# Trunk step on one core: in the MLP's down product, which engine begins the stores and the held back loads, SyncE's loads in the order of the source, and the two resident weight halves in each other's place

## The chip, the cores and the metric

The kernel runs on one core of a Trainium2 chip. The metric is the time of one execution on the device in microseconds (us), lower is better; "before" is the median of three runs. A profiled execution is one further run whose trace gives the rows quoted below. TensorE (PE) does the matmuls, VectorE (DVE), ScalarE (ACT) and GpSimd (POOL) the elementwise work. SyncE (SP) computes nothing: it begins DMA transfers one after the other, and while its next transfer waits for something, every transfer written behind it waits too. GpSimd can begin transfers as well, between its own instructions.

## The reference

One inference step of a two-layer trunk over 1072 columns (16 learned meta tokens, 32 new frames of a running stream, 1024 prompt frames), width 1024, in fp32. Layer 0 mixes with sliding-window attention beside a gated linear attention, layer 1 with a forgetting attention; behind each mixer stands the same MLP. The change touches the MLP alone:

```python
def mlp(h, w_up, w_down):
    u = jax.nn.relu(h @ w_up)
    return (u * u) @ w_down
...
        xp = xp + mlp(rmsnorm(xp, norm_mlp[l]), w_up[l], w_down[l])
        xs = xs + mlp(rmsnorm(xs, norm_mlp[l]), w_up[l], w_down[l])
```

`w_up` is 1024 x 4096 and `w_down` 4096 x 1024, both fp32, and different in each layer.

## The kernel before

**Arithmetic.** Each fp32 operand is split in a rounded high part (`hi_lo`, the cast of ACT at L64) and the rest (the subtraction of DVE at L66); a product is three matmuls, high times high (L75), high times low (L76) and low times high (L77). So the first matmul of a product needs only the cast of its activations, and the second one also their rest.

**Seven products for eight.** Both MLP products are done in a form that replaces a 2 x 2 block product by seven block products of sums and differences. `up` (L930 to L1003) runs through 16 blocks of 64 of the 4096 inner columns of each half, seven products each, and stores after each block seven combinations of the squared results (B11, B21, B22, T1 to T4) from a place in the residual's tile `xT` to a tensor in DRAM, `ud`, with one DMA (L1001). The residual itself was saved to DRAM (`xsave`) before.

**The down product.** `down` (L1010) reads them back. It has seven products n = 0 to 6 (weights A11, S2, S3, A22, A12, S1, S4), and each has two column halves c = 0, 1: 14 passes (n, c), written here (0,0), (0,1), (1,0) and so on. A pass has 16 steps kb of 12 matmuls each, 192 in all. Two steps share one tile of activations u: `acts` loads it (`md_ur`, three buffers) and splits it (`md_u`, four buffers), so a pass has eight such groups, g0 to g7. `ready(at)` makes the activations of a group and of the two behind it. Where the passes with c = 0 accumulate in the PSUM tiles `mu_y` and those with c = 1 in `bank`, the tile's name in a trace tells the two apart.

**Weights.** A11 and A21 stay in SBUF: `k1` and `k2`, four tiles `md_k` of 1 MB each. The other two quarters come in single steps (`md_raw`, 256 KB, three buffers). `weights(n, kb)` combines them and splits the result into `md_w`*kb*, one buffer for each step; for product n+1 it is called in pass (n,1), behind the matmuls of the same step, since these read the buffer it writes. For S2 a step takes two DVE operations (L1032 adds the raw weights to `k2`, L1033 takes `k1` off) and the split. For S3 it takes one (L1037, `k1` less the raw A21), the split, and then ACT's copy of the raw weights to `k1` (L1049), which sets the raw buffer free.

**The start and the held back loads.** Before, `down` begins with the four loads of `k1`, then makes all 16 `md_w` of the first product, and only then the first activations; the scheduler orders this as its model of time finds best. The four loads of `k2` (1 MB each) are spread over pass (0,0), and the restores of `xT` from `xsave` stand at step 4 of each pass with n below 4. Each is held back by a copy of one element by GpSimd (`behind`, L1064), which makes the target tile depend on activations that are made later.

**What sets the order.** Each engine works off its instructions in one fixed order. The program is written in a tile language whose scheduler finds that order with a model of time; only PE follows the order of the source in the MLP (`manual_schedule` in `mlp`). So SP's loads, in the kernel before, stand in the order that the scheduler found for them, and not in that of the loops. At the end of a pass with c the outputs are added to `xT` by DVE (L1120 before, L1124 after the change).

## Time and profile before

| what | value |
|---|---|
| time before, median of 3 runs | 2859.85 us (2859.53 to 2866.35) |
| the profiled execution | 2855.66 us, of which its span 2853.9 us |
| mean granted clock of TensorE | 0.963 |
| TensorE busy | 2631.2 us, 92% of the span |
| VectorE, ScalarE, GpSimd busy | 1888.3, 1264.4, 560.7 us |
| wait of TensorE ahead of the first down product, both layers together | 26.9 us |
| moved by SP's DMA queue, by GpSimd's | 383.62 MB, 7.01 MB |

A row of the timeline gives the start in us from the beginning of the span, the busy time in us, the engine, the line, the operation, the tiles written and read, the number of alike instructions in a row (x4), and in brackets the idle time of the engine just before and what ended it. `SPq` is SP's queue of DMA issues: such a row tells when SP began the transfers, not when they landed. In the view of waits the three numbers behind a pair are the us waited in total, how often, and the longest. In the view of windows come, behind a window, its length, the busy time and number of instructions of PE, PE's weight loads, DVE, ACT and POOL, then the granted clock of TensorE as a share of full speed, the share of the DMA engines, and GB/s.

### The profile page before, as it was taken

What the parts mean: (1) busy time and instruction counts of PE and PEld (TensorE: products, weight loads), DVE (VectorE), ACT (ScalarE), POOL (GpSimd) and SP (SyncE); (2) the same over time, 40 slices, a digit from 0 to 9 for tenths busy, and PEclk for the clock granted to TensorE, in tenths of its full rate; (3) what the DMA queues carried; (4) which work ended last, traced back from release to release, by engine and by line L of the source; (5) the groups of instructions that cost most, each with busy time, mean ns of one, the idle gap of its engine ahead of it and who ended that gap; (6) DMA issues with size and microseconds to landing.
All of it is one profiled execution on the core that took longest, in us unless ns stands there. A gap on an engine that the chain in (4) does not pass through costs nothing.

```text
span 2853.9 us, 49119 instructions
## 1 busy us (share of the span) xinstructions
PE 2631.2 (92%) x18391; PEld 2440.6 (86%) x18391; DVE 1888.3 (66%) x3856; ACT 1264.4 (44%) x2820; POOL 560.7 (20%) x611
## 2 busy tenths in 40 slices
PE   5899988879999899999999978999978999899998
PEld 5788966769999799999789856778768999899998
DVE  5934376687676677578643556778888666677553
ACT  4435454243333345445333346666653333335342
POOL 3423354200000010003110244555520000010000
PEclk9999988899999899999999979999988999999999
DMA  5343241143445577544465374344332444486643
GB/s 192 100 134 104 72 140 45 30 120 101 151 129 164 202 231 218 168 134 121 123 193 168 115 176 127 89 101 102 77 91 79 144 147 144 164 274 205 200 138 105
DMA packets 371286, 393.77 MB, mean 138 GB/s; under 512 B 41503, under 2 KB 300280, under 8 KB 369000
## 3 DMA queue, kind: packets, MB, share of 16 engines
q1 hardware_dynamic: 368552, 383.62, 45.6%
q0 software_dynamic: 2496, 7.01, 0.7%
q8 instruction: 145, 2.38, 0.4%
q14 instruction: 93, 0.76, 0.1%
HBM read 263.94 MB, written 125.48 MB: 136 GB/s over the span
## 4 chain that ended last, share of the span: by engine, by line
PE 63%; issue 16%; DVE 9%; DMA 3%; ACT 2%; SPq 1%; POOL 1%; DVEq 0%; ACTq 0%; POOLq 0%
PE bank L75 11%; PE bank L76 11%; PE bank L77 11%; PE mu_y L77 5%; PE mu_y L76 5%; PE mu_y L75 5%; PE bank L1470 2%; PE bank L1480 1%; PE bank L1481 1%; PE fx_s L1452 1%; PE fx_s L1453 1%; DMA md_raw<-in_w_down 1%; PE bank L257 1%; DVE gl_Q L600 1%; PE b L701 1%
## 5 line engine op out<-in xcount | busy, mean ns | idle before, releaser
L75 PE MATMUL bank<-pj_wh,h 128*128 128x384 f32 (+3 forms) x832 | 298.0, 360 | 9.4 <-ACT pj_wh L64 7.0
L77 PE MATMUL bank<-pj_wh,h 128*128 128x384 f32 (+3 forms) x832 | 295.9, 357 | 6.0 <-DVE h L66 4.8
L76 PE MATMUL bank<-pj_wl,h 128*128 128x384 f32 (+3 forms) x832 | 297.3, 358 | 3.5 <-DVE pj_wl L66 3.5
L75 PE MATMUL mu_y<-md_u,md_w 128*128 128x268 f32 (+1 forms) x896 | 259.4, 289 | 26.9 <-ACT md_u L64 26.9
L76 PE MATMUL mu_y<-md_u,md_w 128*128 128x268 f32 (+1 forms) x896 | 257.8, 288 | 2.4 <-DVE md_u L66 2.4
L77 PE MATMUL mu_y<-md_u,md_w 128*128 128x268 f32 (+1 forms) x896 | 257.3, 287 | 0.0
L75 PE MATMUL bank<-md_u,md_w 128*128 128x268 f32 (+1 forms) x896 | 257.1, 287 | 0.0
L77 PE MATMUL bank<-md_u,md_w 128*128 128x268 f32 (+1 forms) x896 | 255.2, 285 | 0.0
L76 PE MATMUL bank<-md_u,md_w 128*128 128x268 f32 (+1 forms) x896 | 254.9, 285 | 0.0
L64 ACT CAST md_u<-md_ur 128x536 fp32r<-128x536 f32 (+1 forms) x224 | 141.1, 635 | 210.7 <-PE mu_y L77 110.7
L66 DVE TENSOR_TENSOR md_u<-md_ur,md_u 128x536 fp32r<-128x536 f32 (+1 forms) x224 | 157.9, 710 | 114.2 <-ACT md_u L64 113.8
L76 PE MATMUL mu_y<-ho_T,mu_w 128*128 128x268 f32 (+1 forms) x768 | 219.8, 286 | 0.2 <-DVE ho_T L66 0.2
L77 PE MATMUL mu_y<-ho_T,mu_w 128*128 128x268 f32 (+1 forms) x768 | 219.9, 286 | 0.0
L75 PE MATMUL mu_y<-ho_T,mu_w 128*128 128x268 f32 (+1 forms) x768 | 219.2, 285 | 0.0
L75 PEld LDWEIGHTS mu_y<-md_u,md_w 128*128 128x128 f32 x896 | 171.1, 191 | 27.4 <-ACT md_u L64 27.3
L66 DVE TENSOR_TENSOR mu_w<-mu_raw,mu_w 128x512 fp32r<-128x512 f32 x160 | 110.0, 688 | 117.0 <-ACT mu_w L64 117.0
L1283 POOL TENSOR_TENSOR fx_p<-fx_p,sm_den 128x144 f32<-128x144 f32 (+7 forms) x128 | 150.6, 1177 | 181.8 <-DVE sm_den L1282 164.7
L64 ACT CAST mu_w<-mu_raw 128x512 fp32r<-128x512 f32 x160 | 99.2, 622 | 188.6 <-PE bank L77 124.6
L75 PEld LDWEIGHTS bank<-pj_wh,h 128*128 128x128 f32 x832 | 158.8, 191 | 22.3 <-ACT pj_wh L64 7.5
L76 PEld LDWEIGHTS mu_y<-md_u,md_w 128*128 128x128 f32 x896 | 170.9, 191 | 3.5 <-DVE md_u L66 3.4
L77 PEld LDWEIGHTS bank<-pj_wh,h 128*128 128x128 f32 x832 | 158.6, 191 | 17.5 <-DVE h L66 5.1
L76 PEld LDWEIGHTS bank<-pj_wl,h 128*128 128x128 f32 x832 | 159.0, 191 | 16.3 <-DVE pj_wl L66 5.2
(538 smaller groups left out, 8096.2 us busy)
## 6 DMA issues: line engine op xcount, KB each, us to landing
md_raw<-in_w_down SPq DMA_DIRECT2D x160, 256.0 KB
mu_raw<-in_w_up SPq DMA_DIRECT2D x64, 512.0 KB
ud<-xT SPq DMA_DIRECT2D x16, 1876.0 KB
md_ur<-ud SPq DMA_DIRECT2D x112, 268.0 KB
ud<-xT SPq DMA_DIRECT2D x16, 1848.0 KB
md_ur<-ud SPq DMA_DIRECT2D x112, 264.0 KB
md_k<-in_w_down SPq DMA_DIRECT2D x16, 1024.0 KB
fh_ka<-zk SPq DMA_DIRECT2D x32, 260.0 KB
```

Of the source, the lines that this page charges most:

```text
L64: nc.scalar.copy(hi, src)
L66: nc.vector.tensor_tensor(lo, src, hi.bitcast(F32), op=ALU.subtract)
L75: mm(out, ah, bh, start=start, stop=False)
L76: mm(out, ah, bl, start=False, stop=False)
L77: mm(out, al, bh, start=False, stop=stop)
L257: nc.tensor.matmul(*args, start=k == x == 0, stop=k == KB - 1 and x == 1)
L600: eng.tensor_tensor(ov, xv[r, :, :, 1], qv[r, :, :, 1], op=ALU.mult)
L701: nc.tensor.matmul(po[:m, h % 2, h // 2], att[:, h, :m], v[:, P * h:P * h + P], start=True, stop=False)
L1283: nc.gpsimd.tensor_tensor(p[:, :n], p[:, :n], den[:, 0:1].to_broadcast([P, n]), op=ALU.mult)
L1452: nc.tensor.matmul(s[:, a:b], qa[:, qc], ka[:, t0 + a:t0 + b], start=True, stop=False)
L1453: nc.tensor.matmul(s[:, a:b], qb[:, qc], kb[:, t0 + a:t0 + b], start=False, stop=ma >= mb)
L1470: nc.tensor.transpose(pt[:m, P * j:P * j + P], pr[j][:, k0:k0 + m], self.ident)
```

## The change

Six edits, all in the MLP:

1. The 16 stores of `ud` in a layer are begun by GpSimd instead of SP.
2. So are the four held back loads of `k2`.
3. So are the restores of `xT` (16 DMAs over eight passes in a layer).
4. `down` stands under `manual_schedule` for SP and GpSimd: both now follow the order of the source in it.
5. The tiles of `k2` are allocated ahead of those of `k1`, so that each half has the other's place in SBUF, over other operands of `up` than before.
6. `down` begins with the first load of `k1`, the first three loads of activations, and the other three loads of `k1`. Ahead of pass (0,0) only six of the 16 `md_w` are made; the other ten follow within that pass, each six steps ahead of its use.

The matmuls are the same, and in the same order. The diff, without what only shifts lines:

```diff
-                nc.sync.dma_start(self.ud[b // 4][:, b % 4], place[:, b % 2, 1:8, :hw])
+                nc.gpsimd.dma_start(self.ud[b // 4][:, b % 4], place[:, b % 2, 1:8, :hw])
...
-        def load(dst, x, kb, n=1):
+        def load(dst, x, kb, n=1, queue=nc.sync):
             a, c = int(x[1]) - 1, int(x[2]) - 1
-            nc.sync.dma_start(dst, wd[:, c, kb:kb + n, 512 * a:512 * a + 512])
+            queue.dma_start(dst, wd[:, c, kb:kb + n, 512 * a:512 * a + 512])
...
-        for x in range(4):
-            load(k1[x], "A11", 4 * x, 4)
...
-        for kb in range(NP):
+        load(k1[0], "A11", 0, 4)
+        ready(0)
+        for x in range(1, 4):
+            load(k1[x], "A11", 4 * x, 4)
+        for kb in range(6):
             w[0, kb] = weights(0, kb)
...
+                if n == 0 and c == 0 and kb + 6 < NP:
+                    w[0, kb + 6] = weights(0, kb + 6)
                 if n == 0 and c == 0 and kb % 4 == 2:
                     x = k2[kb // 4]
                     behind(x[0:1, 0, 0:1], u)
-                    load(x, "A21", kb - 2, 4)
+                    load(x, "A21", kb - 2, 4, nc.gpsimd)
...
-                        nc.sync.dma_start(self.xT[:, k:k + 2, c0:c1], self.xsave[:, k:k + 2, c0:c1])
+                        nc.gpsimd.dma_start(self.xT[:, k:k + 2, c0:c1], self.xsave[:, k:k + 2, c0:c1])
...
-            k1, k2 = ([kp.tile([P, 4, 512], F32, name=f"md_k{x}{y}") for y in range(4)] for x in (1, 2))
+
+            k2, k1 = ([kp.tile([P, 4, 512], F32, name=f"md_k{x}{y}") for y in range(4)] for x in (2, 1))
...
-            self.down(k1, k2, sb, ps, mid, end)
+            with tc.manual_schedule(engines={mybir.EngineType.SP, mybir.EngineType.Pool}):
+                self.down(k1, k2, sb, ps, mid, end)
```

The order of instructions shows it at three places, all in layer 0 (layer 1 has the same places). First SP's transfers from the end of `up` to the middle of pass (0,0). Before (`md_k_10197` to `10200` is `k1`, `10201` the first tile of `k2`; `ud_6540` to `ud_6543` hold four blocks of the stored results each):

```order
L1018 DMA md_k_10197<-in_w_down 128x4x512
L1018 DMA md_k_10198<-in_w_down 128x4x512
L1018 DMA md_k_10199<-in_w_down 128x4x512
L1018 DMA md_k_10200<-in_w_down 128x4x512
L1058 DMA md_ur<-ud_6540 128x2x268 x2
L1058 DMA md_ur<-ud_6541 128x2x268
L1018 DMA md_raw<-in_w_down 128x512 x2
L1001 DMA ud_6543<-xT 128x3752
L1018 DMA md_raw<-in_w_down 128x512
L1018 DMA md_k_10201<-in_w_down 128x4x512
L1058 DMA md_ur<-ud_6541 128x2x268
```

With the change (`md_k_10201` to `10204` is now `k1`):

```order
L1018 DMA md_k_10201<-in_w_down 128x4x512
L1058 DMA md_ur<-ud_6540 128x2x268 x2
L1058 DMA md_ur<-ud_6541 128x2x268
L1018 DMA md_k_10202<-in_w_down 128x4x512
L1018 DMA md_k_10203<-in_w_down 128x4x512
L1018 DMA md_k_10204<-in_w_down 128x4x512
L1058 DMA md_ur<-ud_6541 128x2x268
L1058 DMA md_ur<-ud_6542 128x2x268 x2
L1058 DMA md_ur<-ud_6543 128x2x268 x2
L1058 DMA md_ur<-ud_6540 128x2x268 x2
L1058 DMA md_ur<-ud_6541 128x2x268
L1018 DMA md_raw<-in_w_down 128x512 x2
```

The store and the load of `k2` have left SP's queue, three activation loads have moved ahead of three quarters of `k1`, and the first raw weights of S2 have moved from behind the third activation load to behind the eleventh.

Second, VectorE at the start of the down product. Before (the `md_w` rows left out are ten further ones like those shown; the last rows belong to S2):

```order
L1000 TENSOR_TENSOR xT<-xT 128x536 x4
L66 TENSOR_TENSOR md_w_10212<-md_k_10197,md_w_10212 128x512
L66 TENSOR_TENSOR md_w_10215<-md_k_10197,md_w_10215 128x512
L66 TENSOR_TENSOR md_w_10218<-md_k_10197,md_w_10218 128x512
L66 TENSOR_TENSOR md_w_10221<-md_k_10197,md_w_10221 128x512
L66 TENSOR_TENSOR md_w_10224<-md_k_10198,md_w_10224 128x512
...
L66 TENSOR_TENSOR md_w_10257<-md_k_10200,md_w_10257 128x512
L66 TENSOR_TENSOR md_u<-md_ur,md_u 128x536 x3
L1032 TENSOR_TENSOR md_k_10201<-md_k_10201,md_raw 128x512 x3
L1033 TENSOR_TENSOR md_k_10201<-md_k_10201,md_k_10197 128x512 x2
```

With the change (again ten `md_w` rows are left out):

```order
L66 TENSOR_TENSOR md_w_10229<-md_k_10201,md_w_10229 128x512
L66 TENSOR_TENSOR md_w_10232<-md_k_10201,md_w_10232 128x512
L66 TENSOR_TENSOR md_w_10235<-md_k_10201,md_w_10235 128x512
L66 TENSOR_TENSOR md_w_10238<-md_k_10201,md_w_10238 128x512
L66 TENSOR_TENSOR md_u<-md_ur,md_u 128x536 x3
L66 TENSOR_TENSOR md_w_10241<-md_k_10202,md_w_10241 128x512
...
L66 TENSOR_TENSOR md_w_10416<-md_k_10204,md_w_10416 128x512
L66 TENSOR_TENSOR md_u<-md_ur,md_u 128x536 x7
L1124 TENSOR_TENSOR xT<-xT,mu_y 128x268 x2
L66 TENSOR_TENSOR md_u<-md_ur,md_u 128x536
L1124 TENSOR_TENSOR xT<-xT,mu_y 128x268 x2
L1032 TENSOR_TENSOR md_k_10197<-md_k_10197,md_raw 128x512 x2
```

The first three splits of activations now stand behind four `md_w` instead of 16, and the first L1032 has moved behind the additions that end pass (0,0).

Third, SP's transfers in pass (1,1), where the weights of S3 are made. Before, from the load for g7 of that pass (`ud_6543`) on; the rows behind it with `ud_6540`, `ud_6540`, `ud_6541`, `ud_6541` are g0 to g3 of pass (2,0):

```order
L1058 DMA md_ur<-ud_6543 128x2x268
L1018 DMA md_raw<-in_w_down 128x512 x2
L1058 DMA md_ur<-ud_6540 128x2x268
L1018 DMA md_raw<-in_w_down 128x512
L1058 DMA md_ur<-ud_6540 128x2x268
L1018 DMA md_raw<-in_w_down 128x512
L1058 DMA md_ur<-ud_6541 128x2x268
L1018 DMA md_raw<-in_w_down 128x512 x2
L1058 DMA md_ur<-ud_6541 128x2x268
L1018 DMA md_raw<-in_w_down 128x512 x2
```

With the change, from the same load on, with the last six of the 16 raw weights of S3:

```order
L1058 DMA md_ur<-ud_6543 128x2x268
L1018 DMA md_raw<-in_w_down 128x512 x2
L1058 DMA md_ur<-ud_6540 128x2x268
L1018 DMA md_raw<-in_w_down 128x512 x2
L1058 DMA md_ur<-ud_6540 128x2x268
L1018 DMA md_raw<-in_w_down 128x512 x2
L1058 DMA md_ur<-ud_6541 128x2x268 x2
```

Of the 16 raw loads of S3, in the first order eight stand behind the load of g2 of pass (2,0) (the first of the two `ud_6541` rows; four of the eight are in the piece shown); in the second all 16 stand ahead of it.

## The prediction

> **What bounds the kernel now.** I read the page first, then TensorE's waits, then the timelines around the largest of them.
>
> ```profile
> PE 2631.2 (92%) x18391; PEld 2440.6 (86%) x18391; DVE 1888.3 (66%) x3856; ACT 1264.4 (44%) x2820; POOL 560.7 (20%) x611
> ```
> ```profile
> PE mu_y L75 <- ACT md_u L64: 26.9, 2, 13.6
> PE mu_y L76 <- DVE md_u L66: 2.4, 4, 1.2
> ```
>
> TensorE is busy for 92% of the span, so only what it waits for can be won. The first of its waits is the one this change touches: 26.9 us in two pieces, one a layer, at the start of the down product.
>
> ```profile
> 972.67 0.29 PE L77 MATMUL bank<-ho_B,mu_w 128*128 128x268 f32 x1
> 986.29 0.59 PE L75 MATMUL mu_y<-md_u,md_w 128*128 128x268 f32 x1 [13.34 <-ACT md_u L64]
> 987.36 0.59 PE L76 MATMUL mu_y<-md_u,md_w 128*128 128x268 f32 x1 [0.47 <-DVE md_u L66]
> ...
> 2485.25 0.28 PE L77 MATMUL bank<-ho_B,mu_w 128*128 128x264 f32 x1
> ...
> 2500.16 0.59 PE L76 MATMUL mu_y<-md_u,md_w 128*128 128x264 f32 x1 [0.47 <-DVE md_u L66]
> ...
> 2512.05 0.39 PE L76 MATMUL mu_y<-md_u,md_w 128*128 128x264 f32 x1 [1.15 <-DVE md_u L66]
> ```
>
> The last matmul of `up` begins at 972.67, the second of `down` (the first that needs VectorE's part of the activations) at 987.36. VectorE, ScalarE and SP say what fills the time between:
>
> ```profile
> 974.22 2.72 DVE L1000 TENSOR_TENSOR xT<-xT 128x536 f32<-128x536 f32 x4
> 976.85 9.82 DVE L66 TENSOR_TENSOR md_w<-md_k,md_w 128x512 fp32r<-128x512 f32 x16
> 986.59 1.96 DVE L66 TENSOR_TENSOR md_u<-md_ur,md_u 128x536 fp32r<-128x536 f32 x3
> 995.10 1.90 DVE L1032 TENSOR_TENSOR md_k<-md_k,md_raw 128x512 f32<-128x512 f32 x3 [6.55 <-issue]
> ...
> 2489.38 7.38 DVE L66 TENSOR_TENSOR md_w<-md_k,md_w 128x512 fp32r<-128x512 f32 x12
> 2499.40 1.94 DVE L66 TENSOR_TENSOR md_u<-md_ur,md_u 128x528 fp32r<-128x528 f32 x3
> ```
> ```profile
> 975.36 2.18 ACT L64 CAST md_w<-md_k 128x512 fp32r<-128x512 f32 x4 [4.93 <-DMA md_k<-in_w_down]
> ```
> ```profile
> 970.03 3.88 SPq L1018 DMA_DIRECT2D md_k<-in_w_down  x4
> 973.95 3.27 SPq L1058 DMA_DIRECT2D md_ur<-ud  x3
> ```
>
> The loads of `k1` begin only at 970.03, since the tiles lie over operands that `up` still reads, so ScalarE casts its first weights at 975.36. And VectorE finishes 16 `md_w` (9.82 us) before it touches the activations.
>
> **The change part by part.**
>
> *The start (new places in SBUF, new order): a gain.* With the change the first load of `k1` and three activation loads lead SP's queue, and four `md_w` instead of 16 stand ahead of the activations on VectorE. I take the loads as landed before `up` ends, so that VectorE sets the start: it leaves L1000 at 976.85 as now, four `md_w` at 9.82/16 = 0.614 us end at 979.31, and the second matmul follows 0.77 us behind the start of the split (987.36 less 986.59), at 980.08. That is 7.28 us earlier. In layer 1: 2489.38 + 4 x 0.615 = 2491.84 for 2499.40, 7.56 us. The wait of 1.15 us at 2512.05 comes from S2's additions that stood in front of an activation; they stand later now, so it goes too. Together 7.28 + 7.56 + 1.15 = **16.0 us** less. If the loads land late, the start falls back towards that of before: the bound is no gain.
>
> Does the half clock of the restart go as well?
>
> ```profile
> 2490.00:2495.00 5.00, 0.00 (x0) 0.00 (x0) 5.00 (x10) 3.72 (x8) 0.00 (x0) 0.54 1.05 386
> 2495.00:2500.00 5.00, 0.59 (x1) 0.29 (x1) 4.78 (x8) 4.46 (x9) 0.35 (x1) 0.50 1.07 383
> 2500.00:2505.00 5.00, 4.84 (x25) 4.84 (x26) 1.34 (x3) 0.12 (x1) 1.59 (x5) 0.59 1.05 390
> ```
>
> The last matmul of `up` ends at about 2485.5 and the granted clock is near a half from 2490 on, so within about 5 us. A wait of some 7 us is left (972.96 to 980.08), so the cold start, (1 - 0.59) x 5 = 2 us in the window behind it, stays: no term.
>
> *The ten other `md_w`, now in pass (0,0).* 10 x 0.614 = 6.1 us of VectorE and as many casts move under the first pass; VectorE is idle there for 6.55 us ahead of 995.10. Hidden, at nothing; without the cover it would be 6.1 us a layer. But what used that time comes later:
>
> *S2's additions: a loss.* SP in source order brings the first raw weights of S2 behind eleven activation loads, and VectorE's order has the first L1032 behind the additions that end pass (0,0), where it began at 995.10, in the middle of the pass. From there to the split of the second activations of pass (1,0), g1, the new order has on VectorE 36 operations of weights, seven of activations and four additions to `xT`.
>
> ```profile
> 1060.24 1.55 DVE L1120 TENSOR_TENSOR xT<-xT,mu_y 128x268 f32<-128x268 f32 x4 [0.46 <-PE mu_y L77]
> ```
> ```profile
> 1037.42 0.29 PE L75 MATMUL mu_y<-md_u,md_w 128*128 128x268 f32 x1
> ...
> 1061.15 0.29 PE L75 MATMUL bank<-md_u,md_w 128*128 128x268 f32 x1
> ```
>
> A pass lasts 1061.15 - 1037.42 = 23.73 us, a group of two steps 2.97. The additions end 0.64 us (1060.24 + 1.55 - 1061.15) into the next pass. Then 36 x 0.614 + 7 x 1.96/3 + 4 x 1.55/4 = 28.2 us: g1 is split at 28.9, and TensorE wants it at 23.73 + 2.97 = 26.7. Late by 2.2; g2 stands six operations on (5 x 0.614 + 0.65 = 3.7 us, against 2.97), 0.7 more. **2.9 us** a layer, from 1 (the shorter step from one start to the next, 0.61, and less waiting) to 5 (raw loads late as well).
>
> *S3's raw weights: the larger loss.* In pass (1,1) each raw buffer is free again only when ScalarE has copied it to `k1` (L1049). Steps 0, 3, 6, 9 and 12 share one buffer:
>
> ```profile
> 1065.40 0.62 ACT L1049 COPY md_k<-md_raw 128x512 f32<-128x512 f32 x1
> ...
> 1071.73 0.62 ACT L1049 COPY md_k<-md_raw 128x512 f32<-128x512 f32 x1
> ...
> 1077.32 0.62 ACT L1049 COPY md_k<-md_raw 128x512 f32<-128x512 f32 x1 [0.22 <-DVE md_w L66]
> ...
> 1083.14 0.62 ACT L1049 COPY md_k<-md_raw 128x512 f32<-128x512 f32 x1 [0.21 <-DVE md_w L66]
> ...
> 1092.11 0.62 ACT L1049 COPY md_k<-md_raw 128x512 f32<-128x512 f32 x1 [0.86 <-DVE md_w L66]
> ```
> ```profile
> 1072.38 0.33 SPq L1018 DMA_DIRECT2D md_raw<-in_w_down  x1
> 1072.96 0.38 SPq L1058 DMA_DIRECT2D md_ur<-ud  x1
> 1074.41 0.33 SPq L1018 DMA_DIRECT2D md_raw<-in_w_down  x1
> 1074.83 0.39 SPq L1058 DMA_DIRECT2D md_ur<-ud  x1
> ...
> 1092.76 0.34 SPq L1018 DMA_DIRECT2D md_raw<-in_w_down  x1
> ```
> ```profile
> 1075.21 0.69 DVE L1037 TENSOR_TENSOR md_k<-md_k,md_raw 128x512 f32<-128x512 f32 x1 [0.45 <-DMA md_raw<-in_w_down]
> ```
> ```profile
> L64 ACT CAST md_u<-md_ur 128x536 fp32r<-128x536 f32 (+1 forms) x224 | 141.1, 635 | 210.7 <-PE mu_y L77 110.7
> ```
>
> Three steps take 5.6 to 6.3 us there (8.97 in the last link, across the end of the pass), TensorE wants three in 3 x 23.73/16 = 4.45. The chain falls behind, and raw load 15 goes out at 1092.76, behind the copy of step 12. Today that hurts nobody: g2 of pass (2,0) was loaded at 1074.83, long ahead. In source order g2 stands *behind* raw load 15, and SP waits there. By this chain: 1092.76 + 0.34, landing 2.83 later (1072.38 to 1075.21, a load of nearly that size), cast and rest 0.64 + 0.65: ready at 1097.2. TensorE wants it at 1061.15 + 23.73 + 2 x 2.97 = 1090.8. Late by 6.4 us. With all links as the first three, (1083.14 - 1065.40)/3 = 5.9, the copy of step 12 begins 3.1 us earlier: late by 3.3. I take **5.0 us** a layer, between the two; with links of the bare parts (2.83 + 0.69 + 0.62 + 0.69 + 0.62 = 5.45) it is 1.5, and 9 where they average 7.3.
>
> By the Trainium skill ("TensorE: Matmul & The Clock Gate", Part 1), TensorE falls back to half its clock after an idle window of about 3.4 us; the clock rows above agree. If S3's delay came as one wait, not over several groups as I expect, that rule would add another cold start, and the sum would be about 2 us a layer higher.
>
> *Stores, `k2` and `xT` on GpSimd.* The copies and issues that the trace has there:
>
> ```profile
> L1064 POOL COPY xT<-md_u x64: 173/174/4267, 987.4 to 2665.3; 1x1 f32<-1x1 f32 x64
> L391 POOL DMA_DIRECT2D zb<-sw_z x36 | 20.4, 566 | 55.6 <-ACT sw_z L387 35.9 <-ACT sw_es L458 12.4 <-ACT sw_z L390 7.3
> ```
>
> An issue costs GpSimd 0.57 us. `k2` and the restores of pass (0,0) are wanted at the end of the pass, some 20 us behind their issue, and a store has one block of `up`. At nothing, then; below nothing hardly, since the other engines do not wait for them now. If each of the seven instructions up to the second restore took the longest 4.27 us, 30 us would stand against 20 of cover: 10 us a layer.
>
> *Other passes.* A22, A12 and S4 free a raw buffer on VectorE, without ScalarE's copy behind it: 2.83 + 0.69 + 0.62 + 0.69 = 4.83 us for three steps against 4.45, so they drift by 2 us over a pass, within the slack of a group (2.97). At nothing; 1 us each if that is used up. Layer 1's output stores by SP wait for work that is done a group earlier: nothing.
>
> *Sum:* -16.0 + 2 x 2.9 + 2 x 5.0 = -0.2 us. From the profiled 2855.66 that is 2855.5; the median of before lies 4.2 above its profile, so I forecast **2860 us**.
>
> **The rivals.**
>
> *The start is won and the lower bounds hold behind it* (faster). For it: before needed no wait in these passes, and the chain's first links are short. Against it: g2 has no way past raw load 15. S2 1.0 and S3 1.5 a layer: -16.0 + 5.0 = -11, **2849**; were SP's order harmless, 2844. Chance 0.28.
>
> *SP's queue blocks S3 for longer* (slower). One place: raw load 15 ahead of g2. With links of 7.5 us (before's last took 8.97) the copy of step 12 begins at 1095.4, g2 is late by 9.7 us, and the sum is -16.0 + 5.8 + 19.4 = +9: **2869**. It decides slower from a mean link of about 7.5 on; below, no change can be told. Against it: part of the last link was the wait for the restore of `xT`, which goes to another queue. Chance 0.15.
>
> *GpSimd starts its transfers late* (slower). The copy of 4.27 us for 0.17 shows that it can be held up while VectorE works. The 10 us above, twice, less the 2.9 of S2 that it covers: +14, **2874**. Chance 0.04. The Trainium skill ("SBUF — State Buffer", the warning on how DVE blocks DMA) says that GpSimd writes the descriptors of its own transfers and can be locked out while VectorE runs certain operations; that speaks for this rival. No run here shows such a delay of a transfer.
>
> *The start is not shortened* (slower): `k1` in its new place waits for `up` as before. The sum is then +15.8: **2876**. Against it: SP's order has the activations ahead of most of `k1` in any case. Chance 0.03.
>
> **How the numbers follow.** The likeliest is the forecast, 0.50: gain and losses cancel to within 0.3% (8.6 us, about what a measurement of this kernel can tell from no change). Faster has 0.28, slower 0.15 + 0.04 + 0.03 = 0.22. The range reaches from the fast rival's 2849, less 3 for a smaller S3, to the slower one's 2869 and 2 us more: 2846 to 2871; the forecast's own, from S2 at 2 to 4 and S3 at 3.3 to 6.4, is 2855 to 2865.
>
> **What would show it.** The first wait on `md_u` should be about 7 us instead of 13.5 in each layer, four `md_w` ahead of the first `md_u`. New waits of TensorE on `md_u` should stand at the beginning of pass (1,0), about 3 us, and at the end of (1,1) and the beginning of (2,0), about 5 us, with SP waiting at an `md_raw` load for L1049 and `md_ur` right behind. If those waits are missing, the kernel is faster by about 0.4%; if the first is still 13 us, or GpSimd's copies and issues take microseconds each, it is slower.

## The result: slower by 1.2%, and where the time went

| | before | after |
|---|---|---|
| median of four runs each | 2863.1 us (2859.53 to 2866.82) | 2896.77 us (2895.45 to 2899.41) |
| ratio, with 95% interval | | 1.0119 [1.01, 1.0137] |
| the profiled execution, its span | 2855.66, 2853.9 us | 2899.41, 2897.3 us |
| mean granted clock of TensorE | 0.963 | 0.963 |

The forecast was 2860 us, and its range ended at 2871. The profiled execution of the changed kernel is the slowest of its four runs and that of before lies below all four of its own, so the two traces differ by 43.4 us where the medians differ by 33.7; the stages below are those of the traces.

The page of the changed kernel and its view of waits (us in total, how often, the longest), the rows that answer to those of before:

```profile
PE 2651.9 (92%) x18391; PEld 2453.2 (85%) x18391; DVE 1884.6 (65%) x3856; ACT 1265.7 (44%) x2820; POOL 643.3 (22%) x683
```
```profile
PE mu_y L76 <- DVE md_u L66: 31.9, 27, 6.5
...
PE mu_y L75 <- ACT md_u L64: 10.7, 12, 2.7
...
PE bank L75 <- ACT md_u L64: 8.0, 7, 1.4
...
PE bank L76 <- DVE md_u L66: 3.7, 9, 1.0
```

Before, TensorE waited for `md_u` 29.3 us in six pieces, all in pass (0,0). Now it is 54.3 us in 55 pieces: two of 6.5 at the start, and 53 of at most 2.7 us, scattered over the passes. And TensorE is busy for 20.7 us more with the same 18391 matmuls (2651.9 for 2631.2). The timeline of TensorE in the changed kernel shows both kinds:

```profile
969.97 0.29 PE L77 MATMUL bank<-ho_B,mu_w 128*128 128x268 f32 x1
...
977.32 0.59 PE L76 MATMUL mu_y<-md_u,md_w 128*128 128x268 f32 x1 [6.55 <-DVE md_u L66]
...
1027.60 0.28 PE L75 MATMUL mu_y<-md_u,md_w 128*128 128x268 f32 x1
...
1029.49 0.39 PE L76 MATMUL mu_y<-md_u,md_w 128*128 128x268 f32 x1 [1.60 <-DVE md_u L66]
...
1055.96 0.29 PE L75 MATMUL bank<-md_u,md_w 128*128 128x268 f32 x1
...
1113.45 0.29 PE L75 MATMUL bank<-md_u,md_w 128*128 128x268 f32 x1
...
2511.37 0.59 PE L76 MATMUL mu_y<-md_u,md_w 128*128 128x264 f32 x1 [6.45 <-DVE md_u L66]
```

The first two rows are the start: 7.35 us from the last matmul of `up` to the second of `down`, where it was 14.69 (972.67 to 987.36). The row at 1027.60 opens pass (1,0), that at 1055.96 pass (1,1) and that at 1113.45 pass (2,1). With the starts of the other passes this table follows; "rest" runs from the start of (2,1) to the next layer's first matmul (layer 0) or to the last matmuls (layer 1).

| stage | layer 0 before, after | difference | layer 1 before, after | difference |
|---|---|---|---|---|
| last matmul of `up` to (0,1) | 41.02, 33.56 | -7.5 | 41.35, 36.21 | -5.1 |
| (0,1) | 23.73, 24.07 | +0.3 | 23.31, 23.36 | 0 |
| (1,0), weights of S2 in use | 23.73, 28.36 | +4.6 | 23.30, 27.96 | +4.7 |
| (1,1) and (2,0), S3 made and in use | 47.47, 57.49 | +10.0 | 46.62, 58.16 | +11.5 |
| rest | 218.09, 229.08 | +11.0 | 225.86, 239.30 | +13.4 |
| sum | | +18.5 | | +24.5 |

Nearly the whole 43.4 us is in these two sums. Up to (0,1) 12.6 us are won, and the passes behind it lose 55.5, more than four times as much.

How waits and busy time share such a loss is seen in the view of windows, (1,1) and (2,0) of layer 0 before and after (length, then busy time and number of PE, PE's weight loads, DVE, ACT and POOL, the granted clock, DMA):

```profile
1061.15:1108.62 47.47, 47.47 (x387) 47.47 (x385) 34.39 (x57) 27.91 (x48) 2.10 (x8) 1.00 0.68 206
```
```profile
1055.96:1113.45 57.49, 52.72 (x386) 51.08 (x385) 35.66 (x60) 28.38 (x48) 5.70 (x12) 0.94 0.58 170
```

Of the 10.0 us, 4.8 are idle (57.49 less 52.72) and 5.2 longer work. The granted clock is 0.94 where it was 1.00, which is 3.4 us of it (0.06 x 57.49). The DMA engines are busy for 0.58 of that time and were for 0.68 before, so it is not a full memory path that holds these passes.

**The loop.** Why does S3 cost 10 us and not 5? ScalarE and SP in pass (1,1) of the changed kernel (the copies at 1059.66, 1067.49 and 1075.04 are those of steps 0, 3 and 6, which share a raw buffer):

```profile
1059.66 0.62 ACT L1049 COPY md_k<-md_raw 128x512 f32<-128x512 f32 x1
...
1066.94 0.64 ACT L64 CAST md_u<-md_ur 128x536 fp32r<-128x536 f32 x1 [0.44 <-DMA md_ur<-ud]
1067.49 0.62 ACT L1049 COPY md_k<-md_raw 128x512 f32<-128x512 f32 x1
...
1073.98 0.64 ACT L64 CAST md_u<-md_ur 128x536 fp32r<-128x536 f32 x1 [1.55 <-DMA md_ur<-ud]
...
1075.04 0.61 ACT L1049 COPY md_k<-md_raw 128x512 f32<-128x512 f32 x1
```
```profile
1063.03 0.42 SPq L1058 DMA_DIRECT2D md_ur<-ud  x1
1068.13 1.37 SPq L1018 DMA_DIRECT2D md_raw<-in_w_down  x2
1069.55 0.43 SPq L1058 DMA_DIRECT2D md_ur<-ud  x1
1070.07 5.94 SPq L1018 DMA_DIRECT2D md_raw<-in_w_down  x2
```

Read it as one chain. The copy at 1067.49 ends at 1068.11, and SP issues the raw load that waited for it at 1068.13. Behind it in SP's queue stands an activation load, issued at 1069.55. ScalarE waits for it to land (1.55 us idle) and casts it at 1073.98. The copy at 1075.04 stands behind that cast on ScalarE; it ends at 1075.65, and only then can SP issue the second of the two raw loads in the last row (1070.07 plus 5.94 less some 0.36 for the issue). So two fixed orders form a loop: on SP the activations wait behind the raw load, on ScalarE the copy that releases the raw load waits behind the activations. Each turn holds the landing of an activation load as well. The links of the chain (steps 0 to 12) are 7.83, 7.55, 7.87 and 6.98 us in layer 0, 8.36, 7.38, 7.68 and 6.67 in layer 1; before they were 6.33, 5.59, 5.82, 8.97 and 6.18, 6.24, 6.2, 7.98. The mean of the first three in layer 0 went from 5.91 to 7.75.

In layer 1's late passes the output stores play the raw load's part (SP, then ScalarE, of the changed kernel):

```profile
2767.75 0.29 SPq L1611 DMA_DIRECT2D out_y_prompt<-so_y  x1
2768.13 4.27 SPq L1058 DMA_DIRECT2D md_ur<-ud  x3
```
```profile
2767.14 0.58 ACT L1610 COPY so_y<-mu_y 116x512 f32<-116x512 f32 x1
2770.64 0.63 ACT L64 CAST md_u<-md_ur 128x528 fp32r<-128x528 f32 x1 [2.92 <-DMA md_ur<-ud]
```

The store at 2767.75 waits for the copy that ends at 2767.72; the activation load behind it goes out at 2768.13, and ScalarE idles 2.92 us for it.

Which edit does it, and is the loop the reason, or is it the moved `md_w` or GpSimd's queue? The experiments take these apart.

### The profile page after: what moved, and what is told of

It reads as the page before. It is cut to its first block, busy times and chain, and to the rows that moved or that the text cites. A ratio compares the mean times of both kernels' runs of the same rounds, so it can differ in the third digit from the quotient of the medians.

```text
span 2897.3 us, 49172 instructions
## 1 busy us (share of the span) xinstructions
PE 2651.9 (92%) x18391; PEld 2453.2 (85%) x18391; DVE 1884.6 (65%) x3856; ACT 1265.7 (44%) x2820; POOL 643.3 (22%) x683
## 5 line engine op out<-in xcount | busy, mean ns | idle before, releaser
L76 PE MATMUL mu_y<-md_u,md_w 128*128 128x268 f32 (+1 forms) x896 | 262.6, 293 | 32.2 <-DVE md_u L66 31.9
L75 PE MATMUL mu_y<-md_u,md_w 128*128 128x268 f32 (+1 forms) x896 | 261.5, 292 | 11.0 <-ACT md_u L64 10.7
L75 PE MATMUL bank<-md_u,md_w 128*128 128x268 f32 (+1 forms) x896 | 259.9, 290 | 8.0 <-ACT md_u L64 8.0
L76 PE MATMUL bank<-md_u,md_w 128*128 128x268 f32 (+1 forms) x896 | 259.2, 289 | 3.8 <-DVE md_u L66 3.7
L77 PE MATMUL mu_y<-md_u,md_w 128*128 128x268 f32 (+1 forms) x896 | 259.0, 289 | 0.0
L77 PE MATMUL bank<-md_u,md_w 128*128 128x268 f32 (+1 forms) x896 | 257.6, 288 | 0.0
L75 PEld LDWEIGHTS bank<-md_u,md_w 128*128 128x128 f32 x896 | 170.9, 191 | 9.6 <-ACT md_u L64 9.5
L75 PEld LDWEIGHTS bank<-pj_wh,h 128*128 128x128 f32 x832 | 159.1, 192 | 21.6 <-ACT pj_wh L64 7.1
L76 PEld LDWEIGHTS bank<-md_u,md_w 128*128 128x128 f32 x896 | 170.9, 191 | 6.4 <-DVE md_u L66 6.0
```

What stands on the lines that cost most here:

```text
L75: mm(out, ah, bh, start=start, stop=False)
L76: mm(out, ah, bl, start=False, stop=False)
L77: mm(out, al, bh, start=False, stop=stop)
```

## The experiments

**1. The changed kernel without its order for SP.** GpSimd still follows the source.

```diff
-            with tc.manual_schedule(engines={mybir.EngineType.SP, mybir.EngineType.Pool}):
+            with tc.manual_schedule(engines={mybir.EngineType.Pool}):
                 self.down(k1, k2, sb, ps, mid, end)
```

> The changed kernel with SP's loads left to the scheduler again; GpSimd alone follows the source. Theory (SP's source order makes a loop: an activation load waits behind a raw load, the raw load waits for ScalarE's copy, and that copy stands behind the cast that waits for the activation load): the start gain of about 7 us a layer stays and the waits from pass (1,0) on go, 2846 us (2840 to 2852). Rival A (VectorE's backlog, from the ten md_w moved into pass (0,0)): the ten are still there, so the waits in pass (1,0) stay, about 4.6 us a layer, 2855 us. Rival B (transfers begun by GpSimd come late or slow the others): nothing changes, 2890 us or more.

Measured: 2848.88 us, ratio to before 0.9951 [0.9937, 0.9966]. Its waits:

```profile
PE mu_y L76 <- DVE md_u L66: 14.8, 7, 6.6
...
PE mu_y L75 <- ACT md_u L64: 3.5, 5, 1.9
```

The start is as short as in the changed kernel, and of the 53 small waits 11 are left, none of them behind pass (0,1): passes (1,0) to (2,0) of layer 0 take 23.80 us each. SP's half of one edit makes the difference between 0.5% faster and 1.2% slower, 1.0119/0.9951 = 1.017, or 48 us.

**2. The kernel before with SP's order alone.** If the loss came from the ten `md_w` moved into pass (0,0), or from GpSimd, it would be absent here.

```diff
-            self.down(k1, k2, sb, ps, mid, end)
+            with tc.manual_schedule(engines={mybir.EngineType.SP}):
+                self.down(k1, k2, sb, ps, mid, end)
```

> The kernel before with one edit: SP follows the order of the source in the down product; all transfers stay on SP, places and start as before. Theory: the whole loss appears without the start gain, some 21 to 25 us a layer: 2905 us (2895 to 2912). Rival A and rival B: nothing to lose here, 2860 us within 8.

Measured: 2910.47 us, 1.0167 [1.013, 1.0204], the same 1.7% on top of before as on top of experiment 1. Its waits:

```profile
PE mu_y L75 <- ACT md_u L64: 33.9, 12, 13.2
PE mu_y L76 <- DVE md_u L66: 20.9, 23, 3.0
```

The start's 13 us are back, and the scatter of small waits is there without any of the other edits. In layer 0 pass (1,0) takes 30.65 us, (1,1) and (2,0) together 57.09, against 57.49 in the changed kernel. So S3's loss comes with SP's order and needs none of the other edits.

**3. The changed kernel with the raw loads begun by GpSimd.** This takes the raw loads, and their waits, out of SP's queue and leaves the order of all else.

```diff
-            load(t.unsqueeze(1), x, kb)
+            load(t.unsqueeze(1), x, kb, 1, nc.gpsimd)
```

> The changed kernel with the single raw weight loads begun by GpSimd as well, so that activation loads are alone on SP and never stand behind a raw load; both engines still follow the source. Theory: the waits at the end of pass (1,1), in (2,0) and later go, those at the start of (1,0) stay (VectorE still begins S2's additions behind pass (0,0)): 2856 us (2848 to 2866). Rival A: 2890 us or more, since VectorE's work is the same. Rival B: 2900 us or more, since 160 more transfers go through GpSimd.

Measured: 2866.15 us, 1.0025 [1.001, 1.0039], just beyond the upper end of what was expected. Passes (1,1) and (2,0) of layer 0 take 23.80 and 23.95 us: S3's loss is gone, as the loop says. So is that of the later passes of layer 0, (3,0), (4,0) and (6,0), which take 23.81 us each. Pass (1,0) is longer instead, 30.05 us, and TensorE waits there for weights. GpSimd in that pass:

```profile
1040.48 0.54 POOL L1018 DMA_DIRECT2D md_raw<-in_w_down  x1 [1.29 <-DVE md_k L1032]
1041.01 6.00 POOL L1064 COPY xT<-md_u 1x1 f32<-1x1 f32 x2
...
1049.32 1.62 POOL L1018 DMA_DIRECT2D md_raw<-in_w_down  x3
```

The raw loads now stand behind GpSimd's copies, which hold back the restores of `xT`: between the one at 1040.48 and the next at 1049.32 none goes out. The same thing in another queue.

**4. The start alone: the kernel before with edits 5 and 6.** Orders of SP and GpSimd are the scheduler's, and all transfers on SP.

```diff
-        for x in range(4):
-            load(k1[x], "A11", 4 * x, 4)
...
-        for kb in range(NP):
+        load(k1[0], "A11", 0, 4)
+        ready(0)
+        for x in range(1, 4):
+            load(k1[x], "A11", 4 * x, 4)
+        for kb in range(6):
             w[0, kb] = weights(0, kb)
...
+                if n == 0 and c == 0 and kb + 6 < NP:
+                    w[0, kb + 6] = weights(0, kb + 6)
...
-            k1, k2 = ([kp.tile([P, 4, 512], F32, name=f"md_k{x}{y}") for y in range(4)] for x in (1, 2))
+            k2, k1 = ([kp.tile([P, 4, 512], F32, name=f"md_k{x}{y}") for y in range(4)] for x in (2, 1))
```

> The kernel before with the two edits on the start alone: the halves' places exchanged, and the new order of the first loads with six md_w ahead; every transfer on SP, in the scheduler's order. Theory and rival B: the start gain alone, 7 to 8 us a layer, 2845 us (2840 to 2850). Rival A: the ten md_w in pass (0,0) cost again what the start wins, 2855 to 2865 us.

Measured: 2848.11 us, 0.9954 [0.9937, 0.997], 11.5 us less than before. Second matmul of `down` 7.35 us behind the last of `up`, as in the changed kernel. This is the forecast's term for the start, less 4.5 us: small waits of 2.02 us and less later in pass (0,0), and passes of 23.80 us for 23.73 (below). In the traces the stretch from the last matmul of `up` to (0,1) is 4.0 and 4.7 us shorter than before in the two layers.

**5. The loop opened from the side of the activations.** The changed kernel, SP in the source's order, but from the third group on the loads of activations are issued two groups earlier; the splits stay where they were.

```diff
+        ur = {}
+
+        def fetch(n, c, g):
+            s = self.STORED.index(self.DOWN[n][1])
+            t = ur[n, c, g] = sb.tile([P, 2, QMAX], F32, name="md_ur", bufs=3)[:, :, :qw]
+            nc.sync.dma_start(t, self.ud[g // 2][:, 2 * (g % 2):2 * (g % 2) + 2, s, qw * c:qw * c + qw])
+
         def acts(n, c, g):
-            s = self.STORED.index(self.DOWN[n][1])
-            t = sb.tile([P, 2, QMAX], F32, name="md_ur", bufs=3)[:, :, :qw]
+            if (n, c, g) not in ur:
+                fetch(n, c, g)
+            t = ur.pop((n, c, g))
             hl = sb.tile([P, 2, 2, QMAX], F32R, name="md_u", bufs=4)[:, :, :, :qw]
-            nc.sync.dma_start(t, self.ud[g // 2][:, 2 * (g % 2):2 * (g % 2) + 2, s, qw * c:qw * c + qw])
...
         def ready(at):
+            if at >= 2:
+                for x in todo[at + 3:at + 5]:
+                    if x not in ur:
+                        fetch(*x)
             for x in todo[at:at + 3]:
```

> The changed kernel with one thing moved in SP's source order: from the third group on, the load of an activation tile stands two groups (5.9 us) earlier, ahead of the raw loads of two groups, while it is split where it was. Theory (SP's order, activation loads behind raw loads): the waits at the end of (1,1), in (2,0) and in later passes go for the most part; the start and the wait in (1,0) stay: 2862 us (2852 to 2872). Rival A (VectorE's work and order): 2885 us or more. Rival C (the raw chain itself is too slow for TensorE, wherever activations stand): waits on md_w take the place of those on md_u, 2880 us or more.

Measured: 2865.51 us, 1.0014 [1.0003, 1.0025], 1% less than the changed kernel with the 23 waits of SP for ScalarE's copies still in place. ScalarE's copies of steps 0, 3 and 6 and a cast between them:

```profile
1061.37 0.62 ACT L1049 COPY md_k<-md_raw 128x512 f32<-128x512 f32 x1 [0.30 <-DVE md_w L66]
...
1065.91 0.64 ACT L64 CAST md_u<-md_ur 128x536 fp32r<-128x536 f32 x1
...
1067.56 0.62 ACT L1049 COPY md_k<-md_raw 128x512 f32<-128x512 f32 x1
...
1072.98 0.62 ACT L1049 COPY md_k<-md_raw 128x512 f32<-128x512 f32 x1 [0.76 <-DVE md_w L66]
```

The cast at 1065.91 waits for no DMA any more, and the links are 6.19 and 5.42 us, 6.68 and 6.65 for the next two. Passes (1,1) and (2,0) of layer 0 take 51.89 us together, 4.4 over before instead of 10.0 (6.5 instead of 11.5 in layer 1). That the links shorten when only the activations' loads come earlier is what shows the loop. The loss that is left is one wait of 1.89 us in (2,0), one of 0.36 and 3.4 us at half clock behind them; it fits the chain's own pace, which the prediction had priced at 5.0. Passes (3,0) and (4,0) take 23.80 us here and (6,0) 27.19. Pass (1,0) shortens too, from 28.36 to 25.41 us.

**6 and 7. The two halves of the start.** Experiment 6 is the kernel before with edit 6 alone (the diff of experiment 4 without its last two lines); experiment 7 is the kernel before with those two lines alone.

> The kernel before with the new order of the start alone: first load of k1, activations, rest of k1, six md_w ahead; the two halves in their old places, SP and GpSimd as before. Theory: VectorE's queue of 16 md_w held the start, so the order wins the most of it even where the loads go out at 970: 2849 us (2845 to 2855). Rival (the late loads, that is the places, held it): 2857 us or more.

> The kernel before with only the places of the two halves exchanged, so that the loads of k1 go out some 15 us earlier; order as before. Theory: 16 md_w still stand ahead of the activations on VectorE, and it is free for them only when up's own work is done: within 3 us of before, 2858 us (2853 to 2862). Rival (the places held it): 2848 us or less.

Measured: the order alone 2860.25 us, 0.9997 [0.9986, 1.0008], a miss; the places alone 2855.21 us, 0.998 [0.997, 0.999], within what was expected. TensorE, and the cast that it waits for, with the order alone:

```profile
975.36 0.59 PE L76 MATMUL mu_y<-md_u,md_w 128*128 128x268 f32 x1 [1.51 <-DVE md_u L66]
...
991.66 0.59 PE L75 MATMUL mu_y<-md_u,md_w 128*128 128x268 f32 x1 [5.35 <-ACT md_u L64]
```
```profile
990.96 0.64 ACT L64 CAST md_u<-md_ur 128x536 fp32r<-128x536 f32 x1 [7.87 <-DMA md_ur<-ud]
```

The start is won (second matmul at 975.36, with the last of `up` at 968.01: 7.35 us), and 15 us later a wait of 5.35 us takes it back. The windows say what is scarce (the last three columns are the granted clock, the share of the DMA engines and GB/s):

```profile
985.00:990.00 5.00, 1.31 (x11) 1.09 (x9) 0.00 (x0) 0.00 (x0) 0.00 (x0) 0.98 0.97 362
990.00:995.00 5.00, 1.57 (x5) 1.27 (x6) 4.76 (x8) 1.92 (x3) 0.71 (x2) 0.50 1.10 361
```

The DMA engines are full (0.97 and 1.10 in the rows shown), and VectorE, ScalarE and GpSimd have nothing to do from 985 to 990, since they wait for bytes; then TensorE restarts at half clock. SP's queue of the two kernels tells why, the order alone first and order with places (experiment 4) second:

```profile
965.37 0.38 SPq L1018 DMA_DIRECT2D md_k<-in_w_down  x1
...
967.62 2.11 SPq L1018 DMA_DIRECT2D md_k<-in_w_down  x3
```
```profile
958.84 0.39 SPq L1018 DMA_DIRECT2D md_k<-in_w_down  x1
...
964.15 3.53 SPq L1018 DMA_DIRECT2D md_k<-in_w_down  x3
```

Here `up` ends at 968.01 and 973.52. With the new places the first 1 MB of `k1` leaves 14.7 us ahead of that end, in the old ones 2.6, and then the 4 MB of `k1` stand in the same full stretch as the next activations. The places alone do not shorten the start either: 16 `md_w` still stand ahead of the activations on VectorE (second matmul 14.58 us behind `up`). Each half is of little use alone; where the 0.2% of the places alone come from, its trace, as long as that of before, does not tell.

**8. A start with weights and activations in turn.** Experiment 4, with VectorE and ScalarE bound to the source's order ahead of pass (0,0): the activations of a group, then its two `md_w`, three times.

```diff
+        with self.tc.manual_schedule(engines={mybir.EngineType.DVE, mybir.EngineType.Activation}):
+            for g in range(3):
+                us[todo[g]] = acts(*todo[g])
+                for kb in (2 * g, 2 * g + 1):
+                    if kb == 4:
+                        for x in range(1, 4):
+                            load(k1[x], "A11", 4 * x, 4)
+                    w[0, kb] = weights(0, kb)
-        ready(0)
-        for x in range(1, 4):
-            load(k1[x], "A11", 4 * x, 4)
-        for kb in range(6):
-            w[0, kb] = weights(0, kb)
```

> The fourth experiment's kernel (places and start order alone) with VectorE and ScalarE in source order for the first three groups: activations of a group, then its two md_w, in turn. The split of the first activations then stands first on VectorE behind up's work instead of behind four md_w: TensorE's second matmul 4 x 0.61 = 2.4 us earlier a layer, of which the half clock and later md_w give some back: 2844 us (2840 to 2848). If ScalarE's or SP's order is what binds there, no gain on that kernel: 2848 us.

Measured: 2858.21 us, 0.9986 [0.9968, 1.0005], a miss, and 10 us more than experiment 4.

```profile
977.42 0.59 PE L76 MATMUL mu_y<-md_u,md_w 128*128 128x268 f32 x1 [4.54 <-DVE md_u L66]
...
1025.73 0.59 PE L75 MATMUL bank<-md_u,md_w 128*128 128x268 f32 x1 [4.46 <-ACT md_u L64]
```

The first wait falls by 2.0 us to 4.54 as it was meant to, and a wait of 4.46 us appears in pass (0,1), which takes 32.76 us. The scheduler found another order for SP here: the activation load that this wait is for stands behind the restores of `xT`, which go out at 1019.62, and leaves at 1020.60, 14 us after the one before it. In experiment 4 four such loads go out between 1004.10 and 1011.89, ahead of these restores. So the start's gain is lost again to a transfer that waits in SP's queue.

**9. The queues alone: the kernel before with edits 1 to 3.** No order is forced.

```diff
-                nc.sync.dma_start(self.ud[b // 4][:, b % 4], place[:, b % 2, 1:8, :hw])
+                nc.gpsimd.dma_start(self.ud[b // 4][:, b % 4], place[:, b % 2, 1:8, :hw])
...
-                    load(x, "A21", kb - 2, 4)
+                    load(x, "A21", kb - 2, 4, nc.gpsimd)
...
-                        nc.sync.dma_start(self.xT[:, k:k + 2, c0:c1], self.xsave[:, k:k + 2, c0:c1])
+                        nc.gpsimd.dma_start(self.xT[:, k:k + 2, c0:c1], self.xsave[:, k:k + 2, c0:c1])
```

> The kernel before with the three moves to GpSimd alone (stores of ud, loads of k2, restores of xT); order, places and start as before, both engines ordered by the scheduler. Theory: no gain and no loss, 2860 us (2854 to 2866), since the first experiment, which has these moves, and the fourth, which has not, came out alike. Rival B (late transfers from GpSimd): 2868 us or more.

Measured: 2860.75 us, 1.0003 [0.9992, 1.0014]: nothing, as expected, to within some 4 us, though a store's issue costs GpSimd 0.77 us (the row below, `x32 | total us, mean ns`) and not 0.57.

```profile
L1001 POOL DMA_DIRECT2D ud<-xT x32 | 24.5, 766 | 691.1 <-DVE xT L976 492.7 <-ACT mu_w L64 141.3 <-ACT md_w L64 37.0
```

Its trace shows one thing that the medians do not: the start is longer, 19.52 and 17.77 us from the last matmul of `up` to the second of `down` in the two layers, for 14.69 and 14.91 before. In layer 0 ScalarE waits 5.63 us for the last quarter of `k1`, 0.57 before. The last store of `ud` now goes out 4.8 us behind the last matmul of `up` instead of 6.7, ahead of those bytes; that it takes their place is not shown.

**10. Layer 1's output stores out of SP's queue.** The changed kernel with the stores of `out_y_prompt` begun by GpSimd.

```diff
-                nc.sync.dma_start(dst[:, 512 * h:512 * h + 512], y[:m])
+                nc.gpsimd.dma_start(dst[:, 512 * h:512 * h + 512], y[:m])
```

> The changed kernel with the output stores of layer 1 begun by GpSimd instead of SP. Theory (whatever waits at the head of SP's queue holds the activation loads behind it, and in passes (4,1) to (6,1) of layer 1 these are the output stores, which wait for ScalarE's copy): pass (4,1) is 5 us shorter and (5,1) some 3, layer 0 is as in the changed kernel: 2888 us (2882 to 2893) against 2897. Rival (SP is held by the raw loads alone): 2897 us.

Measured: 2888.74 us, 1.0097 [1.0074, 1.0119]. TensorE from the start of (2,1) of layer 1 to its last matmuls, here and in the changed kernel:

```profile
2641.90 0.29 PE L75 MATMUL bank<-md_u,md_w 128*128 128x264 f32 x1
...
2867.79 0.38 PE L1609 MATMUL bank<-ident,xT 128*88 128x128 f32 x2
```
```profile
2649.76 0.29 PE L75 MATMUL bank<-md_u,md_w 128*128 128x264 f32 x1
...
2889.06 0.38 PE L1609 MATMUL bank<-ident,xT 128*88 128x128 f32 x2
```

225.89 us for 239.30; before it was 225.86. In the traces the whole 13.4 us of layer 1's late passes goes when the output stores leave SP's queue. The medians differ by 8.0, with intervals that overlap, and the profiled execution here, 2879.61 us, is the fastest of its four, so the size rests on the traces.

**11. The two best parts together.** Experiment 1 with the start of experiment 8, to see whether GpSimd's share of the transfers lets the shorter start be kept.

```diff
-            with tc.manual_schedule(engines={mybir.EngineType.SP, mybir.EngineType.Pool}):
+            with tc.manual_schedule(engines={mybir.EngineType.Pool}):
                 self.down(k1, k2, sb, ps, mid, end)
...
-        ready(0)
+        with self.tc.manual_schedule(engines={mybir.EngineType.DVE, mybir.EngineType.Activation}):
+            for g in range(3):
+                us[todo[g]] = acts(*todo[g])
...
```

> The first experiment's kernel (places, start order, moves to GpSimd, SP by the scheduler) with the interleaved start of the eighth. Theory: the start is 2 us a layer shorter, as there; whether that is kept depends on whether the scheduler puts the fourth activation load far enough ahead. Kept: 2845 us; lost to a wait at the end of pass (0,0) or in (0,1), as there: 2852 to 2858 us.

Measured: 2845.05 us, 0.9949 [0.9931, 0.9968].

```profile
1013.26 0.39 PE L76 MATMUL bank<-md_u,md_w 128*128 128x268 f32 x1 [1.46 <-DVE md_u L66]
```

The start's wait is 4.53 us, and that in pass (0,1) 1.46, where it was 4.46. It is faster than both kernels, by 15.6 us against before; from experiment 1 (0.9951) it cannot be told apart.

## Why the prediction was wrong, step by step

**The start: right.** 7.28 and 7.56 us were forecast, 7.34 and 7.6 measured at the second matmul, with the restart at half clock left in place. The 1.15 us of layer 1 did not come: a wait of 1.88 us stands about where it was. What was not seen is that the gain hangs on both edits, and that part of it comes back later in pass (0,0): by itself the start was worth 11.5 us and not 16 (experiment 4).

**The ten other `md_w` at nothing: right** so far as the runs tell. Experiment 2, without them, loses as much in (1,1) and (2,0), and experiment 4, which has them, takes 23.82 us for (1,0).

**S2's additions, 2.9 us a layer in a range of 1 to 5: 4.6 and 4.7 measured.** The place was right, the beginning of (1,0), and the size was in its bounds, though 1.7 us a layer above the term of the sum. VectorE works without a pause there, as worked out, from 1027.60 to 1040.00 in layer 0; TensorE's waits are 1.60, 1.77 and 0.39 us and begin with g0, not g1. How much of this is VectorE's work alone stays open: in experiment 5, where only the activations' loads come earlier, the pass loses 1.7 us, although the first of S2's additions comes 4.2 us into (0,1) there and 0.2 us in the changed kernel.

**S3's raw weights, 5.0 us a layer: 10.0 and 11.5 measured.** This is the first step that failed. The place and the wait were right: SP waits at a raw load for L1049, and `md_ur` stands behind. But the links of the chain were taken from the trace before (5.9 us for three steps), and they are not a property of the chain: there the activations lay loaded long ahead, and the new order puts one of their transfers into every turn. The four links average 7.56 us (the first three 7.75), and for 7.5 the second rival had worked out 9.7 us a layer. That rival had the mechanism and the price, and got a chance of 0.15; the argument against it (part of the long link was the restore of `xT`) was about another link. But that 9.7 and 10.0 agree is in part luck: the 9.7 is how late one group comes, and of the 10.0 only 4.8 is waiting, spread over (1,1) and (2,0), while half is longer matmuls. The prediction had a further cold start only for one long wait; here two came, each with some 3.4 us at half clock, behind short ones. Whether the longer matmuls add to the chain's delay or lie inside it, since TensorE would have waited otherwise, no run here separates. The rival's own total of 2869 was still too low, since the loop was priced in one place of three.

**The other passes at nothing: wrong, +11.0 us in layer 0's rest.** The working gave them a chain of 4.83 us against 4.45, "within the slack of a group", because the raw buffers come free on VectorE there. In the trace passes (3,0) and (4,0) take 25.68 and 25.23 us for 23.73, and (6,0) of the same layer loses 6.65 us. VectorE, too, stands behind activations in a fixed order. With the raw loads out of SP's queue (experiment 3) these three passes take 23.81 us, and with only the activations' loads earlier (experiment 5) 23.80, 23.80 and 27.19. So the loss needs a raw load ahead of the activations, as the loop does; the links through VectorE were not followed one by one.

**Layer 1's output stores by SP at nothing: wrong, +13.4 us.** The step said that the work they wait for is done a group earlier. It is, but by ScalarE behind a cast that waits for SP: the loop again (experiment 10).

**Stores, `k2` and `xT` on GpSimd at nothing: right** by the medians (1.0003), with a cost per issue of 0.72 to 0.77 us for the 0.57 assumed and the longer start in experiment 9's trace, which the changed kernel does not have.

**The rivals.** Without SP's half of edit 4 the time is 2848.88, the fast rival's 2849, but by luck: passes (1,0) to (2,0) then lose nothing, for which the prediction had 2844, and the start wins less than its 16 us. "GpSimd late" and "the start not shortened" fell. Summed by the traces: the start -7.5 and -5.1, S2 +9.3, S3 +21.5, the rest +24.4 and (0,1) +0.3 give +42.9 of the 43.4 us.

## What to carry to other kernels

A queue that issues transfers in a fixed order and an engine that works in a fixed order can form a loop: look, for every transfer that waits for an engine, whether that engine's next instruction waits for a transfer *behind* it in the same queue. Then a link measured in the old order is no price for the new one; add the landing of every transfer that now stands between a wait and its release, at every place where the queue holds a waiting transfer, not only the worst. And a start that is cut short paid here only where the loads behind it had left before the memory path filled (experiments 4 and 6) and did not wait in the queue behind another transfer (experiments 8 and 11): give them their places in SBUF first.

## What the hardware showed that was not expected

**TensorE can lose its clock over waits of less than 2 us.** Layer 1 of the changed kernel, in pass (0,0), first the timeline, then a window of 1 us with the granted clock in the third column from the right:

```profile
2523.44 0.39 PE L75 MATMUL mu_y<-md_u,md_w 128*128 128x264 f32 x1 [1.88 <-ACT md_u L64]
```
```profile
2525.00:2526.00 1.00, 1.00 (x6) 1.00 (x6) 1.00 (x2) 0.57 (x1) 0.60 (x2) 0.50 0.67 139
```

TensorE was busy to 2521.56, idle for 1.88 us and, from 2523.83, for another 0.35, and behind that its matmuls start 0.22 us apart instead of 0.12 until 2527.84: 3.3 us at half clock, some 1.6 us more, for waits of 2.2. In pass (1,1) of layer 0 waits of 1.31 us (at 1079.84) and 0.36 us (at 1080.59) do the same:

```profile
1080.00:1083.00 3.00, 2.64 (x12) 2.43 (x13) 2.55 (x5) 1.54 (x4) 0.00 (x0) 0.61 0.52 174
```

The Trainium skill ("TensorE: Matmul & The Clock Gate", Part 1) tells of an idle window of about 3.4 us. Here pairs of waits that come to 1.7 us were enough, so the measurement decides: scattered waits can cost clock too. Not all do. In pass (1,0) of layer 0 the clock stays full behind waits of 1.60 and 1.77 us, as this window shows, and in layer 1 it is 1.00 from 2628 to 2637, with a wait of 2.73 us at 2631.52. What decides it is open.

```profile
1027.60:1040.00 12.40, 8.63 (x66) 7.99 (x65) 12.40 (x23) 4.76 (x10) 5.57 (x1) 1.00 0.48 138
```

Where nothing else holds TensorE back, as behind the wait at 2523.44, that time is lost in addition.

**A copy of one element can hold GpSimd for 9.3 us.** In the changed kernel:

```profile
L1064 POOL COPY xT<-md_u x64: 175/177/9324, 976.5 to 2697.3; 1x1 f32<-1x1 f32 x64
```

The median is 177 ns, the longest 9324. VectorE is at work for 9.28 us of that one; that this is the reason is not shown by a run. In experiment 3 such copies hold the raw loads behind them. With only stores, `k2` and restores behind them the time stayed the same (experiment 9, where the longest takes 4.87 us).

**Passes without a wait take 23.80 us instead of 23.73** in layer 0, in every kernel that has edit 6 (23.81 in experiment 3) and in none that lacks it (before, experiments 2, 7 and 9). In layer 1 they take 23.36 instead of 23.31, but for three passes of experiment 3 at 23.31 and 23.32. Over 26 passes that is 1.6 us; what does it is open.
